# Two layers of a diffusion transformer on one core: another clock for the planner of shared steps, and gated-value loads paced to the weights

## The chip, the cores and the metric

The kernel runs on one core of one Trainium2 chip. The time is the device time of one launch in microseconds (us). Before the change three runs gave 3079.08, 3082.59 and 3083.17 us; the median, 3082.59, is the time to be beaten.

The engines of the core that matter here: TensorE (PE, matrix products), VectorE (DVE), ScalarE (ACT), GpSimd (POOL) and SyncE (SP), whose queue issues the DMA transfers. Each engine works through its own list of instructions in order; it waits where an operand or a buffer isn't ready.

## The reference

One image of 1024 tokens and a context of 256 tokens, width 1024, go through two layers. Layer 0 is neighbourhood attention, layer 1 grouped-query attention with normalised queries and keys; each layer ends in a gated feed-forward net (FFN) of hidden width 2816. The context leaves after layer 0.

```python
for i in range(DEPTH):                       # DEPTH = 2
    ... # shifts, scales and gates from silu(c) @ ada_w[i]
    a_l = ada_norm(h, norm_mix[i], sh1_l, sc1_l)
    a_c = ada_norm(hc, norm_mix[i], sh1_c, sc1_c)
    y_l, y_c = neighbourhood or qk-norm attention(a_l, a_c, ...)
    h = h + g1_l * y_l
    h = h + g2_l * swiglu_ffn(ada_norm(h, norm_ffn[i], sh2_l, sc2_l), ffn_w_in[i], ffn_w_out[i])
    if i == 0:
        hc = hc + g1_c * y_c
        hc = hc + g2_c * swiglu_ffn(ada_norm(hc, norm_ffn[i], sh2_c, sc2_c), ffn_w_in[i], ffn_w_out[i])
return rms_norm(h, norm_final)

def rms_norm(x, g):  return x * lax.rsqrt(jnp.mean(x * x, axis=-1, keepdims=True) + EPS) * g
def ada_norm(x, g, shift, scale):  return rms_norm(x, g) * (1.0 + scale) + shift
def swiglu_ffn(h, w_in, w_out):
    a, g = jnp.split(h @ w_in, 2, axis=-1)
    return (jax.nn.silu(a) * g) @ w_out
```

All of it is float32.

## The kernel before

**Splits.** A float32 product is made of three faster ones. Every operand x is split into hi, a cast on ScalarE, and lo = x - hi, a subtraction on VectorE or GpSimd; then hi·hi + hi·lo + lo·hi is summed in PSUM. The three matmuls of the FFN's first product are lines L1455 to L1457, of its second L1698 to L1700, of the second product of the context L1351 to L1353. The casts are L1431 (weights of the first product) and L1189 (the second product's operands); `wh` and `wl` are the halves of a weight, `ah` and `al` those of an activation, `c` a cell of 128x512 that holds any of them. PE passes a 512-column matmul on in about 0.227 us, so each operand has to be cast and subtracted in time.

**The FFN.** Both products are made by the scheme of Strassen: seven block products P1 to P7 (table `PARTS`) in place of eight, over sums of blocks of the operands. The first product goes hidden block by hidden block; P1 and P2 of the first blocks, whose weights need no sums, are put ahead, then P7 and the rest follow. Their results are added up, gated by silu, and the gated values (`FT`, `FA`) are stored to DRAM. The second product runs through P7, P1, P6, P3, P2, P5, P4 in turn (`ORDER2`), 11 hidden blocks each, and reads gated values and weights (`in_fout`) back. The sums of blocks, the subtractions and the results' additions go through one function, `combine`: line L949 where GpSimd does it, L952 where VectorE does. In layer 0 the context's share runs beside it, the second product of the context as a stretch of its own ("ctx2": 528 matmuls of 256 columns), just before the start of layer 1 (its norms and projections, "prologue").

**What sets the order.** The kernel is unrolled when it is built. In the FFNs a planner (class `Lanes`) holds generators, each of which yields the name of the engine that its next step needs: "A" ScalarE, "D" or "D0" VectorE, "G" GpSimd, "GD" whichever of the two comes first, "L" the logarithm and exponential of a norm, "M" a few matmuls, "T" a transfer. The planner keeps a clock of its own, `bg.now`, in ns, and for each engine the time until which it is busy by the planner's costs. `turn` (L636 to L644) moves the clock on by 227 ns, the length of a matmul, offers each engine one step if its busy time has passed, in the order T, M, L, A, D, G, and lets PE go one matmul on (`pump`). The order in which steps are taken is the order of the instructions in each engine's list; the chip then runs these lists without the planner. `both` (L603) is the planner's model of VectorE and GpSimd side by side: an operation that reads two operands from SBUF is put down as longer while the other engine is at one too, and `port` holds the time until which such an operation lasts.

**The steps around the change.** `norm` (L137) sums squares on two accumulators, `ms_sum` (L184) hands them to PE (the matmul with `ones`, L190), ScalarE makes Ln and Exp of it (L177, L179), and `apply_norm` or, in the FFN, L1170 multiplies. `load_h` (L2302) loads the residual stream for the first FFN's norm, `ctx_norm` (L1283) the context's. `load1` (L1370) loads the first product's weights (`in_fin`), `load_w` (L1628) the second's, as cells come free, and `load_t` (L1615) loads gated values into a stock of raw cells (parts of `al` and `ah`) as soon as one is free. All of these transfers are issued by SyncE from one queue. The attention phases follow tables of their own and aren't touched.

Of the kernel before, what the change touches and what calls it, by code (L numbers as in the profile page):

```python
# [72 lines left out]
def _build(tc, nc, I, O, top):  # L73
# [110 lines left out]
    def ms_sum(acc, added, count, n, bank, stop=False):  # L184
        while len(added) < count or max(added) > bg.now:
            yield ""
        ms, free = yield from bank()
        yield "M"
        for i in range(2):
            t.matmul(ms[:, :n], lhsT=ones[:], rhs=acc[i], start=i == 0, stop=stop and i == 1)  # L190
        return ms[:, :n], free

    def apply_norm(tag, src, rs, G, sh, ah, al, tmp):

        left = set(range(KC))

        def split(kc, x, give):
            yield "A"
            s.activation(ah[:, kc, :], x, AF.Identity, bias=sh(kc))
            yield "GD"  # L200
            norm_lo(bg.engine == "G", al[:, kc, :], x, sh(kc), ah[:, kc, :].bitcast(F32))
            left.discard(kc)
            if bg.engine == "G":
                bg.cost = 3.7 * x.shape[1]
            yield from bg.sleep(2000 if bg.engine == "G" else 700)
            give()

        for kc in range(KC):
            x, give = yield from tmp.take("nx", rs.shape[1])
            yield "D0"  # L210
            v.scalar_tensor_tensor(x, src(kc), G(kc), rs, ALU.mult, ALU.mult)
            bg.enter(tag, split(kc, x, give), 800, 1)
        while left:
            yield ""
# [327 lines left out]
    class Lanes:  # L542
# [60 lines left out]
        def both(self, ns):  # L603

            e, o = ("G", "D") if self.engine == "G" else ("D", "G")
            slow = dict(D=2.17, G=1.19)
            left = max(0.0, self.port[o] - self.now)
            beside = min(left, ns * slow[e])
# [3 lines left out]
            self.cost = ns + beside * (1 - 1 / slow[e])  # L612
            self.port[e] = self.now + self.cost

# [20 lines left out]
        def turn(self):  # L635
# [4 lines left out]
            for e in "TMLADG":  # L640
                if self.busy.get(e, 0) <= self.now:
                    self.step(e)
# [374 lines left out]
    class Ffn:  # L1017
# [100 lines left out]
        def src(self, b, k0=0):  # L1118
            return lambda kc: self.h[b][(kc + k0) % KC]
# [166 lines left out]
        def ctx_norm(self, tiles, rings):  # L1286
# [3 lines left out]
            for kc in range(KC):  # L1290
                dma(out=self.c2(kc), in_=H0d[2][:, kc, :])
            at = bg.now + 4000
            tmp = Temps(**tiles)
# [75 lines left out]
        def load1(self):  # L1369

            fin = I[f"fin{self.layer}"]
            self.tasks = {}
            for i, (j, names, _) in enumerate(self.todo):
                q = []
# [240 lines left out]
        def load_t(self):  # L1615

            yield from self.said("feed1")
            for x in ORDER2:
                if x == "P4" and self.layer == 0:
                    self.traw.leave(self.acells1, lambda: self.when.update({"act 1": bg.now}))  # L1620
                for i in range(NP):
                    yield from self.known(("F", i, PARTS[x][1]))
                    cell = yield from self.traw.take()
# [4 lines left out]
        def load_w(self):  # L1628

            yield from self.said("load1")  # L1630
            fout = I[f"fout{self.layer}"]
            for x in ORDER2:
                for i in range(NP):
                    for k, half in self.RAW2[x]:
                        cell = yield from self.raws.take()
                        dma(out=cell, in_=fout[2 * i + k][:, half * 512:half * 512 + 512])
                        self.wq[x, i, k, half] = cell
                        self.when["W", x, i, k, half] = bg.now + 3000
            self.when["load w"] = bg.now

# [661 lines left out]
    def load_h():  # L2302
        for kc in range(KC):
            dma(out=ffn0.h[0][kc], in_=H0d[0][:, kc, :])
            ffn0.at[0, kc] = bg.now + 6000
            yield from bg.sleep(1000)
        ffn0.when["h"] = bg.now
# [319 lines left out]
```

## Time and profile before

One execution was profiled; its own time was 3080.29 us, 2.30 below the median of the runs and within their spread.

| | |
|---|---|
| time, median of 3 runs | 3082.59 us (3079.08 to 3083.17) |
| the profiled execution's own time | 3080.29 us |
| its span | 3078.5 us |
| PE busy | 2936.6 us, 95%, 16460 matmuls |
| VectorE busy | 2339.7 us, 76% |
| GpSimd busy | 1807.9 us, 59% |
| ScalarE busy | 1618.8 us, 53% |
| transfers | 519.05 MB, mean 169 GB/s |
| granted clock of PE, mean | 0.986 |

A busy share of 95% says that PE sets the time, and that what is to be had lies in the places where PE stands still or runs at a lower clock. So the profile is read by places: the windows view gives each engine's busy time in a stretch, and the waits view of PE which operand ended each of its waits. The first FFN begins near 768 us (its norm) and 816 us (its first matmul), its second product near 1370, ctx2 lasts from 1593 to 1676, the prologue of layer 1 follows; the second FFN begins near 2417 and its second product near 2850.

### The profile page before, as it was taken

The numbers are of one execution on the slowest core, as the hardware profiler recorded it, in microseconds if no ns is written. First come the engines' busy times: TensorE is split into PE (matmuls) and PEld (weight loads), VectorE is DVE, ScalarE is ACT, GpSimd is POOL, SyncE is SP. The second block draws the span as 40 slices with busy tenths as digits, with TensorE's granted clock in tenths as the row PEclk, the third lists the DMA queues.
The fourth block names the chain that finished last, engine by engine and source line by source line (L and its number), as shares of the span: only waits on it lengthen the run. The fifth ranks groups of instructions, "written<-read, shape, count | busy, mean of one in ns | idle before, by whom it ended". The sixth has DMA issues, their size and how long they took to land.

```text
span 3078.5 us, 50271 instructions
## 1 busy us (share of the span) xinstructions
PE 2936.6 (95%) x16460; PEld 2511.9 (82%) x16460; DVE 2339.7 (76%) x4291; ACT 1618.8 (53%) x3736; POOL 1807.9 (59%) x1485
## 2 busy tenths in 40 slices
PE   7999999899999999998998899999999989999998
PEld 4888997788788888887878788888888778888786
DVE  7588778775888776567878588899897787666796
ACT  4345555775642222234455488898886622333444
POOL 4246556775685454356776256666644686555775
PEclk8999999999999999999999999999999999999999
DMA  7777777886434554258655523333323333224963
GB/s 262 218 232 236 226 220 225 241 230 210 171 122 159 192 179 168 74 185 298 201 177 188 171 81 96 98 104 105 106 76 121 130 127 127 103 103 152 321 198 113
DMA packets 307173, 519.05 MB, mean 169 GB/s; under 512 B 46433, under 2 KB 112097, under 8 KB 305121
## 3 DMA queue, kind: packets, MB, share of 16 engines
q1 hardware_dynamic: 306912, 515.84, 51.8%
q8 instruction: 131, 2.15, 0.3%
q14 instruction: 130, 1.06, 0.1%
HBM read 389.61 MB, written 120.18 MB: 166 GB/s over the span
## 4 chain that ended last, share of the span: by engine, by line
PE 75%; DVE 10%; DMA 5%; ACT 3%; POOL 3%; issue 2%; SPq 1%; DVEq 0%; POOLq 0%; ACTq 0%
PE pf L1457 9%; PE pf L1455 9%; PE pf L1456 9%; PE T L864 5%; PE o L495 5%; PE pf L1699 4%; PE pf L1700 4%; PE pf L1698 4%; PE ps L767 3%; PE ps L768 3%; PE ps L769 3%; PE S L2235 2%; DMA K<-Kd 2%; PE S L2236 2%; DVE c L952 1%
## 5 line engine op out<-in xcount | busy, mean ns | idle before, releaser
L857 POOL TENSOR_SCALAR Pt<-Pt,rc 128x1280 f32<-128x1280 f32 (+3 forms) x288 | 299.1, 1039 | 389.8 <-ACT pT L872 139.4
L872 ACT CAST pT<-T 128x256 fp32r<-128x256 f32 (+2 forms) x672 | 304.7, 477 | 125.4 <-PE T L864 121.2
L877 DVE TENSOR_TENSOR pT<-T,pT 128x256 fp32r<-128x256 f32 (+2 forms) x672 | 341.7, 534 | 32.9 <-ACT pT L872 32.4
L864 PE MATMUL T<-ident,Pt 128*128 128x128 f32 x1952 | 304.1, 275 | 22.8 <-POOL Pt L857 22.2
L864 PEld LDWEIGHTS T<-ident,Pt 128*128 128x128 f32 x1952 | 236.6, 141 | 78.7 <-POOL Pt L857 34.0
L495 PE MATMUL o<-pT,Vt 128*128 128x256 f32 x1952 | 296.1, 290 | 2.3 <-DVE pT L877 2.2
L767 PE MATMUL ps<-ah,wh 128*128 128x512 f32 (+1 forms) x688 | 261.2, 380 | 5.4 <-ACT ah L430 2.5
L495 PEld LDWEIGHTS o<-pT,Vt 128*128 128x128 f32 x1952 | 254.8, 189 | 9.3 <-DVE pT L877 5.5
L768 PE MATMUL ps<-al,wh 128*128 128x512 f32 (+1 forms) x688 | 251.7, 366 | 3.9 <-POOL al L132 2.2
L769 PE MATMUL ps<-ah,wl 128*128 128x512 f32 (+1 forms) x688 | 251.0, 365 | 2.8 <-DVE wl L336 2.8
L846 ACT ACTIVATE Pt<-S,rc 128x512 f32<-128x512 f32 (+2 forms) x384 | 247.1, 654 | 9.1 <-DVE rc L838 5.8
L949 POOL TENSOR_TENSOR c<-c,c 128x512 fp32r<-128x512 f32 (+1 forms) x120 | 176.0, 1474 | 91.7 <-ACT c L1431 60.0
L2227 DVE TENSOR_REDUCE nm<-S 128x1 f32<-128x512 f32 x256 | 169.6, 682 | 36.4 <-PE S L2236 34.7
L892 POOL TENSOR_TENSOR r<-ob 128x256 f32<-128x256 f32 x144 | 123.8, 859 | 63.1 <-ACT ob L886 57.3
L952 DVE TENSOR_TENSOR c<-c,c 128x512 fp32r<-128x512 f32 (+1 forms) x111 | 128.2, 1168 | 42.3 <-ACT c L1431 24.7
L846 ACT ACTIVATE Pt<-X,rc 128x256 f32<-128x256 f32 x256 | 125.1, 489 | 65.2 <-DVE rc L838 58.5
L949 POOL TENSOR_TENSOR wl<-c,wh 128x512 fp32r<-128x512 f32 x59 | 81.6, 1385 | 120.3 <-ACT wh L1431 113.5
L1431 ACT CAST wh<-c 128x512 fp32r<-128x512 f32 x111 | 68.6, 619 | 157.4 <-POOL c L949 63.9
L769 PEld LDWEIGHTS ps<-ah,wl 128*128 128x128 f32 x688 | 131.2, 191 | 24.4 <-DVE wl L336 3.3
L767 PEld LDWEIGHTS ps<-ah,wh 128*128 128x128 f32 x688 | 131.6, 191 | 18.7 <-ACT ah L430 2.7
L768 PEld LDWEIGHTS ps<-al,wh 128*128 128x128 f32 x688 | 131.7, 191 | 17.3 <-POOL al L132 4.2
L1455 PE MATMUL pf<-c,wh 128*128 128x512 f32 x372 | 144.9, 390 | 0.0
(613 smaller groups left out, 9734.9 us busy)
## 6 DMA issues: line engine op xcount, KB each, us to landing
c<-in_fout SPq DMA_DIRECT2D x119, 256.0 KB, 3.5
wr<-in_wqkv SPq DMA_DIRECT2D x53, 512.0 KB, 4.3
wr<-in_adaT SPq DMA_DIRECT2D x96, 256.0 KB, 3.1
c<-in_fin SPq DMA_DIRECT2D x68, 256.0 KB, 2.9
adaw<-in_adaT SPq DMA_DIRECT2D x64, 256.0 KB, 3.9
wr<-in_wo SPq DMA_DIRECT2D x32, 512.0 KB, 4.2
wr<-in_fin SPq DMA_DIRECT2D x58, 256.0 KB, 2.9
K<-Kd SPq DMA_DIRECT2D x64, 224.0 KB, 4.5
```

The lines of the kernel that those rows point to most:

```text
L495: t.matmul(o_ap, lhsT=u.V[:, kb, :], rhs=u.pT[:, i, :], start=i == 0, stop=i == len(u.blocks) - 1)
L767: t.matmul(ps, lhsT=hi[:, c], rhs=ah[:, kc, :n], start=kc == 0, stop=False)
L768: t.matmul(ps, lhsT=hi[:, c], rhs=al[:, kc, :n], start=False, stop=False)
L769: t.matmul(ps, lhsT=lo[:, c], rhs=ah[:, kc, :n], start=False, stop=kc == KC - 1)
L846: s.activation(u.Pt[:, off:off + u.wid[c]], u.S[c], AF.Exp, bias=u.min, scale=u.sign, accum_out=u.rc[:, 3 + c:4 + c])
L857: g.tensor_scalar(Pt, Pt, u.rc[:, 2:3], 1.0, ALU.mult, ALU.mult)
L864: t.transpose(T[:, i * P:(i + 1) * P], u.Pt[:, (i0 + i) * P:(i0 + i + 1) * P], ident[:])
L872: s.copy(u.pT[:, i0:i0 + n, :P], u.T[c])
L877: v.tensor_tensor(u.pT[:, i0:i0 + n, P:], u.T[c], u.pT[:, i0:i0 + n, :P].bitcast(F32), ALU.subtract)
L1455: t.matmul(ps[:], lhsT=r32(hi[:, c]), rhs=bh, start=k == 0, stop=False)
L1456: t.matmul(ps[:], lhsT=r32(hi[:, c]), rhs=bl, start=False, stop=False)
L1457: t.matmul(ps[:], lhsT=r32(lo[:, c]), rhs=bh, start=False, stop=k == 3)
```

## The change

The planner and a few steps are changed; the arithmetic and the matmuls stay.

- `turn`: an engine may now take a step if it is busy for no more than 226 ns beyond the clock, so that its steps follow one another without waiting for the next multiple of 227 ns. GpSimd takes no step while VectorE, by the plan, is at an operation with two operands from SBUF.
- `both`: the factors of an operation beside the other engine go from 2.17 to 2.25 (VectorE) and from 1.19 to 1.3 (GpSimd), and count from the end of the engine's earlier work. `apply_norm` now tells `both` of its operations.
- `ms_sum` waits 1200 ns more by the plan's clock before it hands the squares to PE.
- `load_h` spaces its loads by 1300 ns instead of 1000 and counts each as there after 7000 instead of 6000; `ctx_norm` counts its own as there after 6000 instead of 4000. In layer 0, `load1` waits until `ctx_norm` has issued its loads.
- `load_t` loads at most three gated values beyond the one for which `load_w` has loaded the weights.

```diff
--- before.py
+++ after.py
@@ -182,7 +182,7 @@
         give()
 
     def ms_sum(acc, added, count, n, bank, stop=False):
-        while len(added) < count or max(added) > bg.now:
+        while len(added) < count or max(added) + 1200 > bg.now:
             yield ""
         ms, free = yield from bank()
         yield "M"
@@ -200,8 +200,9 @@
             yield "GD"
             norm_lo(bg.engine == "G", al[:, kc, :], x, sh(kc), ah[:, kc, :].bitcast(F32))
             left.discard(kc)
+            bg.both((1290 if bg.engine == "G" else 690) * x.shape[1] / 512)
             if bg.engine == "G":
-                bg.cost = 3.7 * x.shape[1]
+                bg.cost += 1.37 * x.shape[1]
             yield from bg.sleep(2000 if bg.engine == "G" else 700)
             give()
 
@@ -209,6 +210,7 @@
             x, give = yield from tmp.take("nx", rs.shape[1])
             yield "D0"
             v.scalar_tensor_tensor(x, src(kc), G(kc), rs, ALU.mult, ALU.mult)
+            bg.both(690 * x.shape[1] / 512)
             bg.enter(tag, split(kc, x, give), 800, 1)
         while left:
             yield ""
@@ -603,14 +605,15 @@
         def both(self, ns):
 
             e, o = ("G", "D") if self.engine == "G" else ("D", "G")
-            slow = dict(D=2.17, G=1.19)
-            left = max(0.0, self.port[o] - self.now)
+            slow = dict(D=2.25, G=1.3)
+            now = max(self.now, self.busy[e])
+            left = max(0.0, self.port[o] - now)
             beside = min(left, ns * slow[e])
             more = min(left * (slow[o] - 1), beside * (1 - 1 / slow[o])) if left else 0.0
             self.busy[o] += more
             self.port[o] += more
             self.cost = ns + beside * (1 - 1 / slow[e])
-            self.port[e] = self.now + self.cost
+            self.port[e] = now + self.cost
 
         def at(self, after, fn):
             heapq.heappush(self.events, (self.now + after, next(self.seq), fn))
@@ -638,7 +641,7 @@
             while self.events and self.events[0][0] <= self.now:
                 heapq.heappop(self.events)[2]()
             for e in "TMLADG":
-                if self.busy.get(e, 0) <= self.now:
+                if self.busy.get(e, 0) <= self.now + 226 and not (e == "G" and self.port["D"] > max(self.now, self.busy["G"])):
                     self.step(e)
             self.pump(1 / 3)
 
@@ -1289,7 +1292,8 @@
             yield from self.said("h")
             for kc in range(KC):
                 dma(out=self.c2(kc), in_=H0d[2][:, kc, :])
-            at = bg.now + 4000
+            at = bg.now + 6000
+            self.when["h2"] = bg.now
             tmp = Temps(**tiles)
             tmp.rings = rings
             G, sh = self.norm2
@@ -1370,6 +1374,8 @@
 
             fin = I[f"fin{self.layer}"]
             self.tasks = {}
+            if self.layer == 0:
+                yield from self.said("h2")
             for i, (j, names, _) in enumerate(self.todo):
                 q = []
                 for u in "a" if names == ["P1", "P2"] else "ag":
@@ -1615,10 +1621,14 @@
         def load_t(self):
 
             yield from self.said("feed1")
+            while not hasattr(self, "seen"):
+                yield ""
             for x in ORDER2:
                 if x == "P4" and self.layer == 0:
                     self.traw.leave(self.acells1, lambda: self.when.update({"act 1": bg.now}))
                 for i in range(NP):
+                    while self.seen + 3 < ORDER2.index(x) * NP + i:
+                        yield ""
                     yield from self.known(("F", i, PARTS[x][1]))
                     cell = yield from self.traw.take()
                     dma(out=cell, in_=self.Fd[i][PARTS[x][1]])
@@ -1628,7 +1638,7 @@
         def load_w(self):
 
             yield from self.said("load1")
-            fout = I[f"fout{self.layer}"]
+            fout, self.seen = I[f"fout{self.layer}"], 0
             for x in ORDER2:
                 for i in range(NP):
                     for k, half in self.RAW2[x]:
@@ -1636,6 +1646,7 @@
                         dma(out=cell, in_=fout[2 * i + k][:, half * 512:half * 512 + 512])
                         self.wq[x, i, k, half] = cell
                         self.when["W", x, i, k, half] = bg.now + 3000
+                    self.seen += 1
             self.when["load w"] = bg.now
 
         RAW2 = dict(P7=((0, 0), (0, 1)), P6=((1, 1),), P4=((1, 1),), P1=((0, 0),), P2=((1, 0),), P5=((0, 1), (1, 1)), P3=((1, 0),))
@@ -2302,8 +2313,8 @@
     def load_h():
         for kc in range(KC):
             dma(out=ffn0.h[0][kc], in_=H0d[0][:, kc, :])
-            ffn0.at[0, kc] = bg.now + 6000
-            yield from bg.sleep(1000)
+            ffn0.at[0, kc] = bg.now + 7000
+            yield from bg.sleep(1300)
         ffn0.when["h"] = bg.now
 
     def columns(G, sh, w):
```

What this does to the lists of instructions, at three places. In all of them the changed kernel's line numbers are shifted: L949 (`combine` on GpSimd) is L952 there, and L952 (on VectorE) is L955; L1698's neighbours and the loads keep their meaning. PE's list has the same matmuls in nearly the same order.

First GpSimd in ctx2, from its first `combine` there on. `c`, `rope` and `xn`, `pl` are cells; L131 and L132 apply the norm of layer 1. Before, over some 120 matmuls:

```order
L949 TENSOR_TENSOR c_16795<-rope,c_16794 128x512
L949 TENSOR_TENSOR c_11550<-c_10548,c_16792 128x512
L949 TENSOR_TENSOR c_11552<-c_10549,c_11551 128x512
L681 TENSOR_TENSOR wl<-wr,wh 128x512
L131 TENSOR_SCALAR xn<-xn,modA_83 128x512
L132 TENSOR_TENSOR al_16863<-xn,ah_16862 128x512
L949 TENSOR_TENSOR c_16792<-c_10548,c_11555 128x512
L131 TENSOR_SCALAR xn<-xn,modA_83 128x512
L132 TENSOR_TENSOR al_16863<-xn,ah_16862 128x512
L144 TENSOR_TENSOR ph<-ph,sq 128x512
L949 TENSOR_TENSOR c_11553<-c_10547,c_16794 128x512
```

and after, over some 260 matmuls:

```order
L131 TENSOR_SCALAR pl<-pl,modA_83 128x512
L132 TENSOR_TENSOR al_16841<-pl,ah_16840 128x512
L952 TENSOR_TENSOR c_16798<-c_10547,c_16797 128x512
L131 TENSOR_SCALAR xn<-xn,modA_83 128x512
L132 TENSOR_TENSOR al_16841<-xn,ah_16840 128x512
L131 TENSOR_SCALAR xn<-xn,modA_83 128x512
L132 TENSOR_TENSOR al_16841<-xn,ah_16840 128x512
L952 TENSOR_TENSOR c_16796<-c_10547,c_11556 128x512
L952 TENSOR_TENSOR c_16795<-c_10549,c_11555 128x512
```

Most of the subtractions have gone to VectorE. In ctx2 `combine` falls from 23 to 5 on GpSimd and rises from 36 to 54 on VectorE, and all of GpSimd's instructions there from 41 to 11. The same holds elsewhere: from the first matmul of the first product to the first P7, `combine` goes from 36 to 7 on GpSimd and from 35 to 61 on VectorE in the first FFN, and from 36 to 10 and from 42 to 65 in the second. In all, 376 instructions leave GpSimd.

Next SyncE at the start of the first FFN's second product; `al` and `ah` are raw cells, `FA` and `FT` gated values, `in_fout` weights, `H0d` the residual stream. Before, the last of 19 loads of gated values in a row and what follows:

```order
L81 DMA al_15179<-FA_9_1215 128x512
L81 DMA ah_15178<-FA_10_1222 128x512
L81 DMA ah_15178<-FT_0_1155 128x512
L81 DMA ah_15178<-FT_1_1162 128x512
L81 DMA ah_15178<-FT_2_1169 128x512
L81 DMA ah_15178<-FT_3_1176 128x512
L81 DMA ah_15178<-FT_4_1183 128x512
L81 DMA ah_15178<-FT_5_1190 128x512
L81 DMA ah_15178<-FT_6_1197 128x512
L81 DMA rope<-in_fout 128x512
L81 DMA c_10550<-in_fout 128x512
L81 DMA c_15473<-H0d_122 128x512
```

and after:

```order
L81 DMA al_15214<-FT_10_1224 128x512
L81 DMA al_15214<-FA_0_1152 128x512
L81 DMA rope<-in_fout 128x512
L81 DMA c_10549<-in_fout 128x512
L81 DMA al_15179<-FA_3_1173 128x512
L81 DMA c_15444<-H0d_122 128x512
L81 DMA rope<-in_fout 128x512
L81 DMA c_10550<-in_fout 128x512
L81 DMA al_15179<-FA_4_1180 128x512
L81 DMA al_15179<-FA_5_1187 128x512
L81 DMA c_15462<-H0d_122 128x512
L81 DMA c_10547<-in_fout 128x512
```

The weights no longer stand behind the whole row of gated values; one or two of these come before each.

Last ScalarE early in the first FFN's first product, where the norm of the second half of the tokens makes its Ln (L177) and Exp (L179) and the context its silu (L1322, in the changed kernel L1326); an ACT_TABLE_LOAD loads a table of functions. Before:

```order
L1431 CAST wh<-wr 128x512
L177 ACTIVATE c_10548<-pf_10553,eps 128x512
L179 ACTIVATE c_10548<-c_10548 128x512
L1322 ACT_TABLE_LOAD
L1322 ACTIVATE c_10503<-pf_10555 128x256
L1431 CAST wh<-wr 128x512
```

and after:

```order
L1326 ACT_TABLE_LOAD
L1326 ACTIVATE c_10503<-pf_10554 128x256
L1437 CAST wh<-wr 128x512
L177 ACT_TABLE_LOAD
L177 ACTIVATE c_10548<-pf_10553,eps 128x512
L179 ACT_TABLE_LOAD
L179 ACTIVATE c_10548<-c_10548 128x512
L1437 CAST wh<-rope 128x512 x2
```

Ln and Exp have fallen behind the silu, and each of them now has a table load ahead of it; a fourth table load stands ahead of the next silu (L1523). Before, Ln and Exp stood 30 and 33 matmuls after the first of the product and the silu at 49; after, the silu at 49, Ln at 68 and Exp at 79.

## The prediction

> **What bounds the kernel now.** I read the page's totals first, then the windows view through the two FFNs, then PE's waits in the windows that are not full.
>
> ```profile
> span 3078.5 us, 50271 instructions
> PE 2936.6 (95%) x16460; PEld 2511.9 (82%) x16460; DVE 2339.7 (76%) x4291; ACT 1618.8 (53%) x3736; POOL 1807.9 (59%) x1485
> ```
>
> PE sets the time: 141.9 us of the span are its idle time. The windows (stretch, its length, then busy time of each engine with its instructions, granted clock, transfers) tell where that lies in what the planner orders:
>
> ```profile
> core 0: us, PE busy (x) PEld busy (x) DVE busy (x) ACT busy (x) POOL busy (x), PEclk, DMA share, GB/s
> 768.00:822.00 54.00, 46.36 (x180) 34.36 (x180) 42.83 (x52) 34.53 (x67) 28.07 (x20) 0.91 0.59 207
> 816.00:872.00 56.00, 55.85 (x353) 50.29 (x353) 49.65 (x52) 35.30 (x65) 43.73 (x28) 1.00 0.31 102
> 868.00:886.00 18.00, 13.69 (x64) 11.29 (x63) 16.65 (x15) 6.88 (x12) 15.95 (x10) 0.81 0.32 102
> 924.00:1386.00 462.00, 462.00 (x2419) 398.46 (x2418) 316.45 (x552) 134.08 (x229) 224.02 (x164) 1.00 0.47 159
> 1398.00:1416.00 18.00, 9.76 (x34) 7.27 (x34) 6.97 (x5) 6.55 (x12) 7.18 (x5) 0.81 1.05 390
> 1593.00:1676.00 83.00, 70.73 (x532) 65.21 (x531) 77.45 (x65) 48.21 (x82) 71.95 (x47) 1.00 0.64 206
> 2417.00:2460.00 43.00, 42.82 (x189) 35.11 (x188) 37.81 (x35) 31.67 (x55) 35.88 (x23) 1.00 0.23 80
> 2455.00:2480.00 25.00, 13.81 (x46) 10.31 (x45) 24.45 (x18) 9.65 (x17) 24.05 (x15) 0.73 0.19 65
> 2550.00:2800.00 250.00, 250.00 (x1104) 207.08 (x1103) 166.82 (x201) 77.35 (x128) 131.47 (x96) 1.00 0.31 109
> 2850.00:2880.00 30.00, 26.52 (x114) 20.85 (x113) 22.43 (x18) 10.42 (x19) 19.34 (x13) 1.00 1.02 369
> ```
>
> In the long stretches PE is full (462.00 of 462, 250.00 of 250): there no order of VectorE and GpSimd can save anything. A 512-column matmul costs 250.00/1104 = 0.227 us there. Against that pace 768 to 822 loses 54 - 180 x 0.227 = 13.1 us, 1398 to 1416 10.3, 2455 to 2480 14.6, 2850 to 2880 4.1; each contains the lower clock after a stop (0.73 to 0.91). PE's waits in these windows (who waited, for whom: total, times, longest):
>
> ```profile
> PE pf L190 <- DVE c L144: 7.5, 3, 4.7
> PE pf L1455 <- ACT wh L1431: 3.4, 1, 3.4
> PE pf L1457 <- DVE wl L952: 0.9, 1, 0.9
> PE pf L1698 <- ACT wh L1189: 7.7, 1, 7.7
> PE pf L1353 <- DVE c L952: 6.6, 7, 1.7
> PE pf L1455 <- ACT wh L1431: 9.2, 1, 9.2
> ```
>
> In this order they belong to the first norm (768), the first P7 (868, two rows), the second product (1398), ctx2 (1593) and the second FFN's first P7 (2455).
>
> **What an operation costs.** VectorE and GpSimd, first apart, then side by side (start, duration):
>
> ```profile
> 846.80 0.68 DVE L952 TENSOR_TENSOR al<-c,ah 128x512 fp32r<-128x512 f32 x1
> 847.40 0.68 DVE L952 TENSOR_TENSOR sq<-sq,pf 128x512 f32<-128x512 f32 x1
> ...
> 860.24 1.29 POOL L949 TENSOR_TENSOR al<-c,ah 128x512 fp32r<-128x512 f32 x1
> ...
> 866.14 1.75 POOL L949 TENSOR_TENSOR wl<-rope,wh 128x512 fp32r<-128x512 f32 x1
> 866.66 1.77 DVE L952 TENSOR_TENSOR wl<-rope,wh 128x512 fp32r<-128x512 f32 x1
> ```
>
> Alone a VectorE operation takes 0.60 (start to start) to 0.68 us; beside GpSimd 1.77, so a GpSimd operation costs VectorE 1.77 - 0.68 = 1.09 us while doing one step itself. Two steps side by side take 1.77, two on VectorE alone 1.2 to 1.36. That speaks for the main part of the change: VectorE does the work of both nearly as fast as both. The Trainium skill ("SBUF — State Buffer", section "SBUF: two separate sides") goes further: the pair of ports is locked for a whole instruction and the other engine stands. By that rule the pair would take 0.68 + 1.29 = 1.97, the trace has 1.77; each GpSimd operation that stays would cost 1.29 in place of 1.09, in the term of ctx2 below 2 us.
>
> **Term 1, ctx2.** Its matmuls have 256 columns; the first and the last of ten consecutive ones:
>
> ```profile
> 1600.02 0.28 PE L1351 MATMUL pf<-c,c 128*128 128x256 f32 x1
> ...
> 1601.09 0.28 PE L1351 MATMUL pf<-c,c 128*128 128x256 f32 x1
> ```
>
> 1.07/9 = 0.119 us each; 528 take 62.8 us, the stretch lasted 83 and VectorE was busy for 77.45 of it, GpSimd for 71.95. By the order VectorE has 90 instructions there after (63 before), six of them 256 wide, and GpSimd 11 (41 before). At 0.60 to 0.68 the 84 wide ones take 50.4 to 57.1, the six some 2.5 (by half the width), and eleven GpSimd operations add 11 x 1.09 = 12.0: 64.9 to 71.6, just above PE's 62.8. Gain 11.4 to 18.1; I take **13**, nearer the slow end, as the operands come from ScalarE and transfers too. None, if VectorE stays at the mean of the row below (47.03/36 = 1.31 us).
>
> **Term 2, the first P7 of each FFN.** What each engine's `combine` did until then:
>
> ```profile
> 816.00:878.00 62.00, 40.65 (x36) 1.00 0.30 97
> 2417.00:2468.00 51.00, 36.01 (x33) 0.97 0.20 67
> 1593.00:1676.00 83.00, 47.03 (x36) 1.00 0.64 206
> ...
> 816.00:878.00 62.00, 47.99 (x30) 1.00 0.30 97
> 2417.00:2468.00 51.00, 43.88 (x27) 0.97 0.20 67
> ...
> 876.52 0.50 PE L1455 MATMUL pf<-ah,wh 128*128 128x512 f32 x1 [3.41 <-ACT wh L1431]
> 2468.98 0.79 PE L1455 MATMUL pf<-ah,wh 128*128 128x512 f32 x1 [9.16 <-ACT wh L1431]
> ```
>
> (three rows of VectorE's L952, then two of GpSimd's L949.) In the first FFN 66 such steps lie before P7, and by the order 7 stay on GpSimd. VectorE then has 59, eight multiplications of the norm, which cost the same, and some 4.7 us of small ones: 67 x 0.60 to 0.68 + 4.7 + 7 x 1.09 = 52.5 to 57.9 us, that is from 816 until 868.5 to 873.9. PE comes there at about 873. So most of the 3.4 + 0.9 goes, part of it gives way to gaps in VectorE's list; I take **4**, with bounds of 0 and 7.7 (the wait and 18 us at a clock of 0.81, 3.4 us). In the second FFN 60 steps, 10 of which stay: 58 x 0.60 to 0.68 + 10 x 1.09 = 45.7 to 50.3, from 2417 until 2462.7 to 2467.3, against 2468.98: gain 1.7 to 6.3 of wait and with a shorter stop some of the clock's loss; I take **5**, bounds 0 and 14.6.
>
> **Term 3, the second product's start.** SyncE issued 18 loads of gated values in a row (one stands at the dots), and only then the weights:
>
> ```profile
> 1390.72 5.01 SPq L81 DMA_DIRECT2D al<-FA  x10
> ...
> 1396.96 5.09 SPq L81 DMA_DIRECT2D ah<-FT  x7
> 1402.40 0.33 SPq L81 DMA_DIRECT2D rope<-in_fout  x1
> 1407.86 0.62 ACT L1189 CAST wh<-rope 128x512 fp32r<-128x512 f32 x1 [13.79 <-DMA rope<-in_fout]
> ```
>
> The cast waited 13.79 us for a weight that stood behind them, and the transfers were full (1.05, 390 GB/s). After, loads alternate. P7 of the second product needs 11 gated tiles and 22 weights, 256 KB each: 8.65 MB in 11 x 12 x 0.227 = 30 us, 288 GB/s, below the 390 seen. So the 10.3 us go but for a remainder: **8.5**, bounds 0 (the transfers stay full) and 10.3. Behind a paced load on SyncE stand later weights and `H0d`; they are issued earlier, not later. In the second FFN (2850, 1.02 of the transfers' share) the same: **2.5** of 4.1.
>
> **Term 4, the first norm.** The sums of squares are handed over later: five more projection groups, 15 matmuls or 3.4 us, go ahead of the first hand-over, into a wait of 4.7. Against it the last of eight loads is 7 x 0.3 = 2.1 us later. **5** with the clock, bounds -4 and 8.
>
> ScalarE gets three more table loads near 822:
>
> ```profile
> 821.86 0.69 ACT L177 ACTIVATE c<-pf,eps 128x512 f32<-128x512 f32 x1
> 822.57 0.63 ACT L179 ACTIVATE c<-c 128x512 f32<-128x512 f32 x1
> 823.22 1.28 ACT L1322 ACT_TABLE_LOAD   x1
> ```
>
> 3 x 1.28 = 3.85 us of ScalarE, 35.30 of 56 busy there: hidden. The Ln stands 38 matmuls later, 38 x 56/353 = 6 us; what waits for it is VectorE's norm of the second half, in front of T3, and VectorE has subtractions to do until then. I count nothing; if it isn't hidden, the 4 of term 2 turns into -6. The Trainium skill ("ScalarE: Activation LUTs", "What ACT_TABLE_LOAD costs") adds a drain of 1.38 us to each switch, 8.0 us in all; the rows show the load 0.02 us behind the Exp, no drain before it.
>
> **Sum.** 13 + 4 + 5 + 8.5 + 2.5 + 5 = 38. What one place gains the next can take back: PE comes to the prologue of layer 1 and to the dense stretches sooner, while VectorE has more to do. In ctx2 five of GpSimd's eight pairs for layer 1's norm went to VectorE, and the prologue itself is ordered as before. I take off a fifth, 8: **30**. From the profiled execution's 3080.29 that gives **3050**; from the median it is 32.6 less, and the difference of 2.3 is within the runs' spread.
>
> **Rivals.**
> (a) Only the transfers gain (term 3): VectorE alone is as much of a bound as the pair was, since each remaining GpSimd step costs 1.09 and operands come late anyway. For it: in term 2 the slow bounds leave 2 us. Against it: 1.2 to 1.36 for two steps against 1.77. 3080.3 - 11 = **3069**.
> (b) The stalls only move, or GpSimd still runs beside VectorE because the chip doesn't keep the planner's times: **3078**. For it: the planner's port is its own clock. Against it: 376 instructions have left GpSimd whatever the times.
> (c) Slower: VectorE becomes the bound of the second products. Of these, the first FFN's takes 926 matmuls, 210 us of PE, and VectorE gets 244 instructions there after (161 before; GpSimd 17 after, 104 before). At 0.68 that is 166 + 17 x 1.09 = 184, with 26 to spare; it decides from a mean of 0.79 us on, and at 0.85 costs 244 x 0.85 + 18.5 - 210 = 16 us. Half as much again in the second FFN, where no context lies between, less the 11 of term 3: 3080 + 24 - 11 = **3093**. For it: the mean of 1.31 in ctx2. Against it: that mean was measured beside GpSimd, busy for 71.95 of 83.
>
> **How the numbers follow.** Forecast 0.60, (a) 0.20, (b) 0.09, (c) 0.11. The likeliest's own range is 3035 to 3062 (the bounds of terms 1 to 4, not all at one end). The whole range, 3032 to 3076, takes in (a) and leaves out (b), (c) and gains of over 48. About 0.2%, 6 us, is what a measurement can tell: faster 0.81, the same 0.09, slower 0.10.
>
> **What would show it.** Ctx2 in at most 72 us with L952's work at about 0.7 us each; no wait of PE at L1698 behind ACT's cast near the second product's start, and weights issued before the last gated values; both first P7 with waits under 5 us; the norm's hand-over without its 4.7. Wrong if VectorE's mean stays above 0.85 with GpSimd nearly idle, if waits of PE appear in the windows that are full now, or if the Exp at 822 ends PE's wait for P7.

## The result, and the profile after

The changed kernel takes 3031.99 us (median of four runs, 3030.41 to 3034.7) against 3081.99 for the kernel before on the same chip: a ratio of 0.984, with a 95% interval of 0.9823 to 0.9857, 50 us less. The forecast was 3050, 32.6 below the median; the measured time lies at the lower edge of the range (3032). The profiled execution took 3030.41 us. The direction and the places were foretold, the size was not: the forecast had 30 of the 50 us, and the measured time lies below the likeliest's own range of 3035 to 3062.

The page's totals of the changed kernel:

```profile
span 3028.6 us, 50110 instructions
PE 2917.2 (96%) x16460; PEld 2503.2 (83%) x16460; DVE 2304.4 (76%) x4659; ACT 1621.8 (54%) x3739; POOL 1245.6 (41%) x1109
```

VectorE has 368 instructions more than before and is busy 35 us less; GpSimd has 376 fewer and is busy 562 us less. So an operation of VectorE has become shorter on the average; whether that comes of what GpSimd no longer does beside it, the experiments test. The windows of the changed kernel at the places that the prediction named (columns as there; the places have moved with what was gained ahead of them):

```profile
core 0: us, PE busy (x) PEld busy (x) DVE busy (x) ACT busy (x) POOL busy (x), PEclk, DMA share, GB/s
864.00:882.00 18.00, 16.06 (x80) 13.41 (x79) 17.03 (x27) 9.38 (x17) 8.14 (x5) 0.91 0.39 129
918.00:1379.00 461.00, 461.00 (x2415) 397.54 (x2415) 320.65 (x602) 134.21 (x230) 149.83 (x110) 1.00 0.47 160
1385.00:1403.00 18.00, 18.00 (x81) 14.89 (x80) 14.83 (x24) 10.02 (x19) 5.17 (x4) 1.00 1.04 384
1575.00:1645.00 70.00, 67.30 (x537) 65.07 (x536) 62.83 (x92) 48.03 (x84) 17.59 (x11) 1.00 0.73 245
1642.00:1682.00 40.00, 37.26 (x226) 32.16 (x224) 23.93 (x45) 21.00 (x46) 10.88 (x11) 1.00 0.25 80
2422.00:2447.00 25.00, 22.38 (x92) 18.07 (x91) 21.52 (x31) 10.14 (x18) 11.23 (x9) 0.93 0.27 95
2800.00:2830.00 30.00, 30.00 (x134) 24.83 (x133) 23.03 (x39) 14.80 (x24) 1.32 (x1) 1.00 1.00 364
```

The starts of both second products are full now (18.00 of 18, 30.00 of 30), with the transfers still at 1.04 and 1.00 of their share: they were never short, they came in the wrong order. Ctx2 is down to 70 us. At the second FFN's first P7 there is still a gap, with 92 matmuls in 25 us where there were 46. PE's waits of the changed kernel in 760 to 900 (first norm and first P7), then in 2368 to 2530:

```profile
PE pf L190 <- DVE c L144: 5.2, 2, 2.6
PE pf L1461 <- ACT wh L1437: 1.5, 1, 1.5
...
PE pf L1461 <- ACT wh L1437: 2.6, 1, 2.6
```

At the first P7s the casts are waited for 1.5 us (3.4 before) and 2.6 us (9.2); in the second products PE waits for nothing.

### The profile page after: what moved, and what is told of

Read it like the earlier page. It is cut to its first block, busy times and chain, and to the rows that moved or that the text cites. A ratio compares the mean times of both kernels' runs of the same rounds, so it can differ in the third digit from the quotient of the medians.

```text
span 3028.6 us, 50110 instructions
## 1 busy us (share of the span) xinstructions
PE 2917.2 (96%) x16460; PEld 2503.2 (83%) x16460; DVE 2304.4 (76%) x4659; ACT 1621.8 (54%) x3739; POOL 1245.6 (41%) x1109
## 3 DMA queue, kind: packets, MB, share of 16 engines
q14 instruction: 127, 1.04, 0.1%
## 4 chain that ended last, share of the span: by engine, by line
PE 77%; DVE 9%; DMA 5%; ACT 3%; POOL 3%; issue 2%; SPq 1%; DVEq 0%; POOLq 0%; ACTq 0%
PE pf L1461 9%; PE pf L1462 9%; PE pf L1463 9%; PE T L867 5%; PE o L497 5%; PE pf L1711 5%; PE pf L1710 5%; PE pf L1709 5%; PE ps L770 3%; PE ps L771 3%; PE ps L772 3%; DMA K<-Kd 2%; PE S L2246 2%; PE S L2247 2%; DVE pT L880 1%
## 5 line engine op out<-in xcount | busy, mean ns | idle before, releaser
L952 POOL TENSOR_TENSOR c<-c,c 128x512 f32<-128x512 f32 (+1 forms) x63 | 92.6, 1472 | 248.7 <-DVE c L955 89.5
L955 DVE TENSOR_TENSOR c<-c,c 128x512 fp32r<-128x512 f32 (+1 forms) x166 | 131.3, 804 | 48.5 <-ACT c L1437 34.6
L1437 ACT CAST wh<-c 128x512 fp32r<-128x512 f32 x112 | 68.9, 618 | 166.9 <-PE pf L1462 66.8
L1461 PE MATMUL pf<-c,wh 128*128 128x512 f32 x376 | 146.5, 390 | 0.0
L1462 PE MATMUL pf<-c,wh 128*128 128x512 f32 x376 | 146.5, 390 | 0.0
```

Of the source, the lines that this page charges most:

```text
L1461: t.matmul(ps[:], lhsT=r32(hi[:, c]), rhs=bh, start=k == 0, stop=False)
L1462: t.matmul(ps[:], lhsT=r32(hi[:, c]), rhs=bl, start=False, stop=False)
```

## The experiments

Whole times scatter more than the stages do: attention 0, whose instructions stand in the same order in all of these kernels, took between 745.5 and 755.2 us in their profiled executions. So the kernels are compared by stages, cut at starts of PE's matmuls: attention 0 ends with the start of its last group of products with V (L495), norm and first product of the first FFN with the first L1698, its second product with the first L1351, ctx2 with the last L1353, the prologue with the first product of queries and keys in layer 1, attention 1 as attention 0; the second FFN's norm ends with the first L1455, its first product with its first L1698, the second with the start of the last group of matmuls, so that it takes in a wait of the final norm. All in us, from one profile each, taken on several chips. "Rest" is all but attention 0; "raster" stands for the old clock, by which a step is only taken at multiples of 227 ns.

| kernel | norm + first product | second product | ctx2 | prologue | second FFN: first product | its second product | rest |
|---|---|---|---|---|---|---|---|
| before | 69.5 + 556.3 = 625.8 | 221.9 | 83.0 | 81.0 | 435.7 | 220.7 | 2333.0 |
| changed | 63.4 + 552.7 = 616.0 | 211.2 | 69.2 | 81.0 | 425.1 | 214.8 | 2280.6 |
| changed, again | 64.5 + 549.7 = 614.3 | 211.2 | 68.5 | 81.6 | 423.8 | 214.8 | 2279.2 |
| pacing alone | 68.4 + 556.7 = 625.1 | 211.4 | 82.9 | 81.0 | 435.5 | 217.1 | 2318.9 |
| rule alone | 66.0 + 558.2 = 624.2 | 224.7 | 67.7 | 105.9 | 430.8 | 227.2 | 2343.8 |
| clock alone | 69.8 + 553.1 = 622.8 | 219.4 | 85.1 | 83.5 | 431.2 | 221.9 | 2328.1 |
| clock and rule | 68.9 + 547.3 = 616.2 | 221.0 | 77.4 | 82.5 | 424.8 | 220.2 | 2305.3 |
| changed, no rule | 69.9 + 559.7 = 629.6 | 211.2 | 80.2 | 83.5 | 432.7 | 215.1 | 2316.5 |
| changed, raster | 62.6 + 560.5 = 623.0 | 211.3 | 67.4 | 105.8 | 432.3 | 219.7 | 2322.3 |
| changed, old norm times | 66.0 + 547.2 = 613.3 | 211.2 | 70.3 | 82.5 | 423.7 | 214.8 | 2280.8 |
| changed, VectorE alone | 62.6 + 552.9 = 615.4 | 211.2 | 67.7 | 85.2 | 426.7 | 214.8 | 2285.4 |
| changed, no 1200 ns | 66.6 + 547.5 = 614.1 | 211.2 | 70.4 | 82.5 | 423.7 | 214.8 | 2281.1 |
| changed, old factors | 63.6 + 550.1 = 613.7 | 211.2 | 77.3 | 83.5 | 425.3 | 214.8 | 2288.3 |
| changed, silu late | 66.4 + 548.4 = 614.8 | 211.2 | 69.6 | 81.1 | 425.1 | 214.8 | 2280.0 |

The first theory (T) was the prediction's: three parts that don't depend on one another. Its rivals were that stalls only move (R1) and that the finer clock does the work (R2). Four kernels tell these apart.

**Pacing alone.** To the kernel before, only

```diff
+            while not hasattr(self, "seen"):
+                yield ""
...
+                    while self.seen + 3 < ORDER2.index(x) * NP + i:
+                        yield ""
...
+                    self.seen += 1
```

> The kernel before with nothing but the pacing of the gated-value loads. Theory T (three parts that do not depend on one another: the GpSimd rule gives ctx2 and both first P7, some 28 us; the pacing gives the starts of both second products, 10.6 + 4.9 = 15.5 us; the new norm times some 4): 3082 - 15.5 = 3066 us, no wait of PE for ACT's cast at the second product's start, ctx2 still 83 us. Rival R1 (stalls only move: PE is early at ctx2 and waits there for the VectorE/GpSimd pair, so that most of it is given back): 3075 us or more, ctx2 some 90 us.

3073.09 us against 3088.01 (0.9956, 0.9939 to 0.9972). The second product loses 10.5 us and nothing else changes before the second FFN: ctx2 takes 82.9. The whole is 14.9 us faster, where T had 15.5. Its windows view where the weights used to be late:

```profile
1406.00:1424.00 18.00, 18.00 (x81) 14.92 (x80) 14.27 (x16) 10.30 (x19) 14.83 (x12) 1.00 1.05 385
```

R1 falls. T holds for the first FFN; in the second, pacing gives 3.6 of 5.9 us (220.7 to 217.1). The rest comes with clock and pacing together: clock alone or with the rule doesn't give it (221.9, 220.2), the changed kernel without the rule has it (215.1), and on the raster it does not (219.7).

**The rule alone.** To the kernel before, only

```diff
-                if self.busy.get(e, 0) <= self.now:
+                if self.busy.get(e, 0) <= self.now and not (e == "G" and self.port["D"] > max(self.now, self.busy["G"])):
```

> The kernel before with only the rule that GpSimd takes no step while VectorE, by the plan, reads two operands from SBUF; the 227 ns raster and the old cost factors stay. By the order GpSimd then has 5 of the subtractions in ctx2 (before 23, the changed kernel 5), 8 before the first P7 (36, 7) and 11 before the second FFN's (36, 10). T: ctx2 near 70 us, both first P7 early, 3082 - 28 = 3054 us, the second product's starts as before (waits near 8 us). Rival R2 (it is the finer clock that matters, since with the raster each VectorE step is held to a multiple of 227 ns in the order): 3070 us or more.

3094.14 us against 3088.01: slower, 1.0023 (1.0013 to 1.0033), and here T and R2 both miss a part: T's 3054 by 40 us, and R2 the gain in ctx2. Ctx2 does what T said (67.7 us), but the prologue behind it takes 105.9 instead of 81.0 and gives back more than all of it. The longest of PE's waits in that kernel from 1655 to 1780, then its windows over ctx2 and behind it:

```profile
PE o L190 <- DVE y L144: 16.4, 2, 10.8
```

```profile
1594.00:1663.00 69.00, 66.28 (x532) 65.51 (x530) 58.06 (x75) 43.42 (x74) 26.26 (x19) 0.98 0.74 243
1663.00:1700.00 37.00, 19.12 (x107) 15.55 (x108) 25.20 (x36) 15.55 (x32) 14.06 (x13) 0.72 0.12 39
```

PE waits twice for sums of squares of the norm of layer 1, 5.6 us for those of the second half of the tokens and 10.8 for the context's: VectorE does 36 instructions in 37 us there, with PE busy for half of it, and the context's sums stand behind five of the second half's eight multiplications. By the order, 16 of the norm's multiplications (L211) stand behind ctx2, before and in the changed kernel 8. So ctx2 was short also because its work had been put off.

**The clock alone.** To the kernel before, only `self.now + 226` in that line.

> The kernel before with only the finer clock (a step may be taken up to 226 ns ahead), without the rule for GpSimd. By the order GpSimd keeps 22 of 23 subtractions in ctx2, 34 of 36 and 33 of 36 before the first P7s, but 77 of 93 and 74 of 93 in the second products. T: ctx2 stays above 78 us, 3072 to 3082 us. R2: 3054 us with ctx2 near 70.

3080.53 us against 3088.01 (0.9977, 0.9968 to 0.9986). Ctx2 stays at 85.1, R2 falls for it; there are small gains before the second product and in the second FFN (431.2 for 435.7).

**The changed kernel without the rule.** Only the `and not (...)` taken out.

> The changed kernel without the rule for GpSimd (finer clock, new cost factors, pacing and norm times stay). GpSimd has 23 subtractions in ctx2 again, 32 and 31 before the first P7s. T: it loses the 28 us of ctx2 and the two first P7s: 3032 + 28 = 3060 us, with the starts of the second products still free of waits. R2: within 8 us of 3032.

3066.68 us against 3088.01 (0.9928, 0.9904 to 0.9953): 2316.5 us of rest against 2280.6, 36 us more. The losses stand where T has them: 80.2 in ctx2, 629.6 and 432.7 in the first products. So by the stages the rule is worth 36 us in the changed kernel and costs 11 alone (by the ratios to the kernel before on the same chip some 27, near T's 28, and 7). And with GpSimd back in ctx2 (67.02 us busy in the window of 80), VectorE's `combine` there takes 1.22 us each again, as the prediction's 1.31 before:

```profile
1588.00:1668.00 80.00, 43.74 (x36) 1.00 0.65 214
```

R2 falls here too. The new theory (C), for what the rule loses by itself: on the raster a VectorE step of some 690 ns takes up four turns of 227, 908; with GpSimd barred beside it, the plan has too little room and puts the norm of layer 1 off. The finer clock gives the room back. The rival (K) was that the new cost factors do that.

**Clock and rule**, nothing else changed from before (both edits of that line):

> The kernel before with the finer clock and the GpSimd rule, and nothing else (old cost factors, no pacing, old norm times). Theory C (the rule alone gains in ctx2 and loses 24.8 us in the prologue because on the raster VectorE's steps fall behind in the plan, so that twice as many norm steps of layer 1 are left for after ctx2; the finer clock removes just that): the order has 8 norm multiplications after ctx2 again, so prologue 81 to 84 us, ctx2 67 to 72, second FFN's first product 8 to 11 us shorter, second products as before: 3050 to 3058 us. Rival K (it takes the new cost factors to keep the norm steps in time): prologue still over 95 us, above 3070 us.

3054.74 us against 3086.71 (0.9892, 0.987 to 0.9915). The prologue is back at 82.5, the second FFN's first product at 424.8, with the old factors: C holds, K falls. The expectation for ctx2 was wrong: 77.4 us, not 67 to 72.

**The changed kernel on the raster**, only `+ 226` taken out:

> The changed kernel with the 227 ns raster put back (a step only when the engine's planned work is over); the rule, new factors, pacing and norm times stay. Theory C: the order has 17 norm multiplications after ctx2, so the prologue takes some 105 us against 81 and the whole is 20 to 25 us slower than the changed kernel, about 3055 us. Rival K: the new factors suffice, prologue below 88 us, within 8 us of 3032.

3075.04 us in one run, prologue 105.8, and the same wait (of PE for L144, 16.3 us) as with the rule alone. C holds a second time for the prologue, K falls; but the whole, which C put at 3055, is missed by 20 us. By the rest it is some 42 us worse, since the first products lose 7 us each and the second FFN's second product 4.9 too.

**The changed kernel with the old cost factors** asks what makes up the 8 us of ctx2:

```diff
-            slow = dict(D=2.25, G=1.3)
+            slow = dict(D=2.17, G=1.19)
...
-            bg.both((1290 if bg.engine == "G" else 690) * x.shape[1] / 512)
...
-                bg.cost += 1.37 * x.shape[1]
+                bg.cost = 3.7 * x.shape[1]
...
-            bg.both(690 * x.shape[1] / 512)
```

> The changed kernel with the old cost factors (2.17 and 1.19, norm steps not told to the model). Theory N (the factors move the norm steps of layer 1 off GpSimd in ctx2, where clock and rule alone took 77.4 us against 69.2): ctx2 75 to 79 us, prologue 81 to 83, 6 to 10 us slower than the changed kernel. Rival Z (they do nothing once the rule is there; the difference in ctx2 comes from the pacing, which brings PE there earlier): ctx2 68 to 71 us, within 3 us.

3038.41 us against 3088.09 (0.985, 0.9817 to 0.9883). The interval takes in the changed kernel's ratio; the stages show the difference: ctx2 77.3 us, the prologue 83.5, all else within 2.5 us of the changed kernel. PE's waits in ctx2:

```profile
PE pf L1355 <- DVE c L953: 6.0, 4, 2.3
PE pf L1355 <- POOL c L950: 2.4, 4, 1.3
```

N holds by its size, Z falls. By the order GpSimd has 9 subtractions in ctx2 here, 5 with the new factors, and in the traces 12 instructions of layer 1's norm there instead of 6. Whether it takes the factors, or that the planner is told of the norm's steps, isn't separated.

**The shared steps given to VectorE alone** (in the norms, the splits, the weights and the gating, at six places, of this kind):

```diff
-            yield "GD"
+            yield "D"
             combine(r32(lo), x, hi, ALU.subtract)
```

> The changed kernel with the shared steps of the FFNs' operands, sums and norms given to VectorE alone. Theory P (each GpSimd step that is left costs VectorE 1.09 us, more than the 0.60 to 0.68 it saves): as fast or up to 8 us faster, 3024 to 3032, with the first P7s no later. Rival V (VectorE is the bound and GpSimd's shared steps fill only its gaps, so taking them away lengthens its list): 5 to 25 us slower, P7 waits of over 5 us.

3033.78 us against 3086.71 (0.9827, 0.9805 to 0.985), as a whole the same as the changed kernel: neither P nor V. By the stages ctx2 gains 1.5 us and the prologue loses 4.2, and the rest is 4.8 longer (6.2 against the changed kernel's second profile). So what GpSimd has left is no burden on the whole; in the prologue it helps by some 4 us, in single profiles. `combine` on VectorE in ctx2, with GpSimd idle, takes 0.65 us each:

```profile
1573.00:1641.00 68.00, 38.64 (x59) 1.00 0.77 252
```

**The norm times.** First all of them taken back:

```diff
-        while len(added) < count or max(added) + 1200 > bg.now:
+        while len(added) < count or max(added) > bg.now:
...
-            at = bg.now + 6000
+            at = bg.now + 4000
...
-            if self.layer == 0:
-                yield from self.said("h2")
...
-            ffn0.at[0, kc] = bg.now + 7000
-            yield from bg.sleep(1300)
+            ffn0.at[0, kc] = bg.now + 6000
+            yield from bg.sleep(1000)
```

> The changed kernel without the new norm times (1200 ns before the hand-over, loads counted later, first-product weights after the context's loads). Theory S (as predicted, these bridge the norm's wait): the stretch before the first FFN's first matmul takes 67 to 69 us in place of 63.4, 3036 us. Rival G (the gain of 5.8 us there comes from the GpSimd rule, which showed 3.2 us alone): 63 to 66 us, 3030 to 3034.

3036.4 us against 3086.71 (0.9827, 0.9806 to 0.9848). The norm's stretch takes 66.0, between S and G, but the first product takes 547.2 instead of 552.7, and the two together 613.3, less than the changed kernel's 616.0 and 614.3. The order shows a difference in between: Ln and Exp of the second norm stand 27 and 30 matmuls after the first, ahead of the context's silu, as before the change. That led to theory L, that the silu in front of them and the table loads cost the first product 5 us. Then only the 1200 ns:

> The changed kernel with only the 1200 ns of ms_sum taken back (load times and everything else stay). By the order Ln and Exp of the first FFN's second norm stand 27 and 30 matmuls after the first again, ahead of the context's silu, with one table load there instead of four. Theory L (the place of Ln and Exp behind the silu and its three more table loads costs 5 to 6 us before the first P7, as the kernels with it took 552.7 to 560.5 us for the first product and those without it 547.2 to 553.1): first product 547 to 548 us, no wait at the first P7, start of the first FFN 63 to 66 us, in all 3 to 6 us faster than the changed kernel, 3026 to 3030 us. Rival H (it is the load times that lengthen the first product, as the weights come after the context): 552 to 554 us, no faster than 3031.

3032.87 us against 3088.09 (0.9822, 0.9808 to 0.9837): first product 547.5 as L had it, against H, norm 66.6, together 614.1, and no faster as a whole. So the difference in the two stretches goes with the 1200 ns; the load times show no effect. Last L by itself, the silu held until the Exp has been taken:

```diff
             sa = self.run[j, "sa"] = yield from self.sa.take()
+            yield from self.said("ln1")
             yield "A"
```

> The changed kernel, in which the context's first silu may only be taken once the Exp of the second norm has been: by the order Ln and Exp stand 53 and 58 matmuls after the first (changed kernel 68 and 79), then the silu at 67 with the one table load there. All the other counts stay as in the changed kernel. Theory L (Ln and Exp behind the silu, with three more table loads, cost some 5 us before the first P7): first product 547 to 550 us in place of 552.7, no wait at the first P7, in all 3 to 6 us less than the changed kernel on the same chip, the start of the first FFN still near 63.4. Rival M (the 5 us came from the norm's earlier hand-over as such; Ln is still 26 matmuls later than in the kernels with 547): 551 us or more and no difference in the whole.

ScalarE in this kernel, and in the changed one:

```profile
828.17 0.68 ACT L177 ACTIVATE c<-pf,eps 128x512 f32<-128x512 f32 x1
828.89 0.63 ACT L179 ACTIVATE c<-c 128x512 f32<-128x512 f32 x1
...
830.05 1.28 ACT L1328 ACT_TABLE_LOAD   x1
```

```profile
821.93 0.61 ACT L1437 CAST wh<-wr 128x512 fp32r<-128x512 f32 x1
822.56 1.28 ACT L177 ACT_TABLE_LOAD   x1
823.85 0.69 ACT L177 ACTIVATE c<-pf,eps 128x512 f32<-128x512 f32 x1
824.56 1.28 ACT L179 ACT_TABLE_LOAD   x1
825.86 0.63 ACT L179 ACTIVATE c<-c 128x512 f32<-128x512 f32 x1
```

3031.26 us against 3085.78 (0.9816, 0.9799 to 0.9833). And the changed kernel beside it:

> The changed kernel once more, beside the one above. 1.6% to 1.8% faster than the kernel before on the same chip; stages as in its first profile (first product 552 to 553 us).

3034.52 us (0.9834, 0.9815 to 0.9854). The wait at the first P7 (1.5 and 0.4 us in the changed kernel) is gone with the silu late, but the first product takes 548.4 where the changed kernel's own second profile has 549.7 (not the 552 to 553 that were expected of it), and norm and first product together take 614.8 and 614.3. The two intervals overlap. So L's mechanism is there with 2 us of wait, its 5 us aren't: the same program took 552.7 and 549.7 us in that stage, and what is won in one of the two stretches has been lost in the other. None of these versions is shown to be faster than the changed kernel.

## Why the prediction was right, and where it was short

**Ctx2 (13).** Measured 13.8 and 14.5. The mechanism stands: `combine` on VectorE in ctx2, by its line, took in the changed kernel

```profile
1575.00:1645.00 70.00, 39.81 (x54) 1.00 0.73 245
2384.00:2434.00 50.00, 40.61 (x60) 0.97 0.26 89
```

(the second row is for the second FFN's start): 0.74 and 0.68 us each, 1.31 and 1.09 before; in ctx2 GpSimd's work fell from 71.95 us to 17.59. One price was too high, the 1.09 us that each remaining GpSimd operation was to cost VectorE. The groups of VectorE in that window:

```profile
L955 DVE TENSOR_TENSOR c<-c,c 128x512 fp32r<-128x512 f32 x35 | 26.2, 760 | 5.5 <-ACT c L1192 4.9 <-PE pf L1356 0.4
L955 DVE TENSOR_TENSOR c<-rope,c 128x512 fp32r<-128x512 f32 x19 | 14.9, 783 | 1.6 <-ACT c L1192 1.4
L212 DVE SCALAR_TENSOR_TENSOR xn<-c,G,rs 128x512 f32<-128x512 f32 x7 | 6.3, 896 | 0.0
```

They are longer than 0.68 by 35 x 0.08 + 19 x 0.10 + 7 x 0.22 = 6.2 us, by this estimate some 0.6 for each of the 11 GpSimd operations of that window, not counting the smaller groups. The other price named there, 1.29, is further off still (and 0.20 more for eleven operations would be 2.2 us, not below 2). The kernel with VectorE alone gains 1.5 us in ctx2, so little hangs on what is left of them.

What the prediction did not see at all is that this term has three conditions. The rule by itself loses 24.9 us in the prologue, the clock gives nearly all of them back, and the factors, with the norm's steps told to the planner, are worth 8 of the 13.8. It treated rule, clock and factors as one edit, which they are in this change.

**The first P7 of the second FFN (5).** This term was mis-sized: 10.6 and 11.9 us. From its own bounds for the wait, 1.7 to 6.3, a middle was taken with "some of the clock's loss". The wait for the cast fell by 6.5 (9.16 to 2.62), and a second one, which the kernel before has in 2417 to 2530, went:

```profile
PE pf L1457 <- DVE wl L952: 2.0, 1, 2.0
```

That is 8.5, more than the bound. What put the bound too low was the price of 1.09 again: with 0.6 the prediction's 58 steps and 10 GpSimd operations end between 2457.8 and 2462.4, an estimate, and PE comes at 2459.8 (2468.98 less 9.16). Of the 3.4 us that the lower clock cost (14.6 less the two waits) some 1.9 went too (of 25 - 92 x 0.227 = 4.1 us that are still lost, 2.62 are the wait), as the granted clock in the window rose from 0.73 to 0.93. The first P7 of the first FFN (4) is in the next term's stage.

**The first norm (5) and the first P7 (4).** Together 9.8 and 11.5 us, against 9. That the size is right is luck for the norm's part, for the cause given for it is not right: clock and rule without the new norm times give 616.2 against 616.0, and the changed kernel without them 613.3. With the new norm times the norm's stretch is 2.6 us shorter (63.4 for 66.0) and the first product 5.5 longer in the first profile; and the kernel with the silu late, which keeps them, has 66.4. On the whole the later hand-over and the later loads gain nothing that these runs show. PE's wait for L144 went from 7.5 to 5.2 us, not by the 4.7 that the fifteen matmuls were to fill.

**The second products (8.5 and 2.5).** Measured 10.7 and 5.9. The first is all that was to be had (10.3 by the count of matmuls); the 1.8 held back for full transfers weren't needed. In the second the pacing gives 3.6, and the clock with it the rest. The prediction lets each of its four losing windows contain a lower clock; that of 2850 to 2880 has 1.00 in its own row.

**ScalarE's table loads (nothing).** Each took the 1.28 us of the row, and the Ln came 2.0 us later than before by its time (823.85 against 821.86), while all ahead of it came some 4 us earlier. With the silu late the first P7 waits no longer, so they were not hidden wholly; what it is worth, at most 2 us of wait, isn't seen in the whole. The drain of 1.38 us per switch that the Trainium skill states ("ScalarE: Activation LUTs", "What ACT_TABLE_LOAD costs") doesn't appear: the cast ahead of the first load starts at 821.93 and takes 0.61, the load starts 0.02 us after its end, and Ln 0.01 after the load's.

**The 8 taken off.** This failed. Nothing was given back: the prologue took 81.0 and 81.6 us after 81.0, attention 1 594.0 and 594.8 after 594.7, the long stretches are as full as before (461.00 of 461). Together: the sum of 38 was short by 5.6 in the second FFN's P7, by 2.2 and 3.4 in the second products, by 0.8 in ctx2, by 0.8 in the first stage, by 1.5 in the second FFN's norm (57.0 to 55.6; 56.6 in the second profile), and 8 were taken off for nothing. With the 30 that makes 52.3, and the rest fell by 52.4; the profiled executions differ by 49.9, as attention 0 took 2.4 us more in the later one. The fear behind the 8 was right for another kernel: with the rule alone the prologue took back 24.9.

**The rivals.** (a), transfers alone, is the kernel with pacing alone: some 15 us by the medians, 14.1 by the stages, where 11 were worked out. (b) didn't come about. (c) is refuted for the second products, which are the same 211.2 and 214.8 us with VectorE doing nearly all shared steps; but something like it lay nearer than its 0.11: on the raster, the same rule makes the kernel slower.

## What to carry to other kernels

When two engines slow each other, handing the slower one's work to the faster is worth most where PE waits for the pair, here in ctx2 and ahead of each first P7; but the order has to be made anew for it, with room on the faster engine, or the work is only put off to a place where PE waits longer. A stall costs its wait and the lower clock behind it, so a term for a stall that goes should hold both. A deduction for what may be taken back needs a place and a price like any other term, and whole times that scatter by almost 10 us in an untouched phase are better compared by stages.

## What the runs showed of the hardware

VectorE's `combine` in ctx2 took the longer, the more GpSimd had to do beside it: 1.31 us with GpSimd busy for 71.95 of 83 us, 1.22 with 67.02 of 80, 0.74 with 17.59 of 70 and 0.65 with none. The same list of instructions for attention 0 took from 745.5 to 755.2 us in the profiled executions, a spread larger than most of the differences studied here; 745.8 and 755.2 were on one chip, and the cause stays open. And a transfer queue that is full (1.05 of the share, 390 GB/s) need not be what PE waits for: after the pacing it was as full (1.04, 384 GB/s), over the same kind of window, with PE at work in all of it.
